# Gated projection: the last four column tiles as block products by seven multiplications, all engines in written order

## The chip, the cores and the metric

One core of a Trainium2 chip runs the whole program. The metric is the device time of one execution in microseconds (us). The engines are TensorE (PE, matrix products), VectorE (DVE, elementwise), ScalarE (ACT, activations, copies and casts), GpSimd (POOL), and the queues that issue DMAs (SP, ACT, POOL). Each engine runs its own instructions in one order and waits on semaphores for the others.

## The reference

One block of a conformer with a state-space branch: 512 tokens of 1024 features, all in float32. Cut to what matters here:

```python
h = rms_norm(x, mix_pre_g[i])
proj = h @ w_in[i]
u_glu, z, xbc, dt_raw, gates = ...           # pieces of proj
val, gt = jnp.split(u_glu + glu_b, 2, axis=-1)
v = val * jax.nn.sigmoid(gt)                 # the gated projection
v = causal_depthwise_conv(v, dw_w, dw_b)     # 31 taps
conv_out = jax.nn.silu(layer_norm(v, ln_g, ln_b)) @ pw_w + pw_b
ssm_out = ssd_branch(z, xbc, dt_raw, ...)    # 8 groups
mixed = (g_conv * conv_out + g_ssm * ssm_out) @ w_out[i]
x = x + rms_norm(mixed, mix_post_g[i])
...                                          # a gated feed-forward part
```

val and gt have 1024 columns each, 8 tiles of 128; the four last tiles of both are what the change touches.

## The kernel before

**Products.** A float32 product is made of three products of a fast type: each operand is split into a high and a low half, and `mm3` (L251 to L260) issues high x high (L253), and the two mixed ones (L255, L259). Activations are held as `hhi`/`hlo` (features x 512 tokens). Weights come in pieces of 128 x 1024 by the SP queue into `raw` (5 buffers), ScalarE casts the high half `whi` (L209), VectorE subtracts the low half `wlo` (L216); for some pieces ScalarE writes the negative high half and a POOL DMA adds the weights onto it in memory (L213, L214).

**Stages on TensorE.** val and glu of tiles 0 to 3 (on x before its normalisation, scaled afterwards by `rb`); z of group 0 with the time steps dt (`pz0`, L529); val and glu of tiles 4 to 7 (`pv4` to `pg7`): eight projections of 8 x 3 matmuls of 512 columns; then eight SSD groups. A group projects x (two tiles, `px`), B and C, transposes x (`pxT`), forms the diagonal product with the decay matrix `L`, the state product (`pSa`, `pSb`, from `xdec` and `BT`) and the part from earlier chunks. After them the gates, the pointwise product of the convolution branch, the output projection and the feed-forward part. The pointwise product and gate-up are already block products: both operands are cut in 2 x 2 blocks, sums and differences of blocks are multiplied, and seven products of 256 columns take the place of eight.

**The convolution.** Each of the 8 gated tiles `v` needs 31 taps into a tile `a`, all on VectorE (L521). They fill VectorE between other work, from a list (`taps`) that the stages draw from by fixed numbers (`TAPS`, `TAPS_GLU`).

**The time steps.** `time_steps` (L446) makes dt on VectorE. `running_sums` (L465) multiplies by a triangle (`pcs`) and by ones (`pend`) on TensorE, then transposes the running sums (`pT`) and writes them to memory (`scr`); `make_L` (L489) reads them back spread over partitions by a POOL DMA, masks them on GpSimd with affine_select (L496), and ScalarE takes 16 exponentials per group (L503).

**Order.** TensorE's and VectorE's order follows the program with edges put in by hand (`not_before`, `issue_after`, `by_table`, `keep_in_program_order`); `by_table` keeps ScalarE's calls in program order where they need tables, so that the 16 exponentials of a group stand together. The gate-up part has written orders for VectorE and ScalarE.

Of the kernel before, what the change touches and what calls it, by code (L numbers as in the profile page):

```python
# [1797 lines left out]
```

## Time and profile before

| | us |
|---|---|
| three runs | 1012.22, 1013.33, 1015.75 |
| median | 1013.33 |
| the profiled execution | 1013.44 |
| its span in the profile | 1011.7 |

The span runs from the first to the last instruction; the 1.7 us beside it lie around the program. The profile's stages by TensorE's start times:

| start us | stage |
|---|---|
| 51.08 | z of group 0 and dt |
| 63.81 | val and glu, tiles 4 to 7 |
| 108.04 | SSD group 0 |
| 129.80 | group 1 |
| 170.04 | group 2 |
| 480.00 | gates, z of the last groups and the end of SSD |
| 600.83 | pointwise product |
| 687 | gate-up |
| 898 | down projection |

A row of the timeline has start, duration, engine, line, operation, out<-in and shape, and in brackets the idle time of the engine before it with what ended it. Durations of pipelined instructions overlap: the cost of one in a full engine is the distance from its start to the next start.

### The profile page before, as it was taken

The page shows a single profiled execution, that of the slowest core. Times are in us where ns is not written, and L with a number is a line of the kernel's source. Part 1 is how long each engine was busy: PE and PEld are TensorE (multiplying, and loading weights), DVE is VectorE, ACT ScalarE, POOL GpSimd, SP SyncE. Part 2 cuts the span into 40 slices and gives each one's busy share as a digit, 9 for nine tenths or more (in the row PEclk, how much of TensorE's full clock was granted, in tenths as well). Part 3 has the DMA queues.
Part 4 walks back from the last instruction along what each step waited for, and adds up shares of the span by engine and source line. Part 5 has one row for each costly group of instructions (what it writes and reads, how often), then busy time and mean ns, then how long its engine had stood idle before and what let it go on. Part 6 is the DMA issues. An engine that isn't in the chain of part 4 may idle for free.

```text
span 1011.7 us, 15883 instructions
## 1 busy us (share of the span) xinstructions
PE 1003.7 (99%) x6152; PEld 877.9 (87%) x6152; DVE 845.7 (84%) x1230; ACT 619.8 (61%) x1045; POOL 105.9 (10%) x138
## 2 busy tenths in 40 slices
PE   9999999999999999999999999999999999999997
PEld 7898889888888888888888889889999999998886
DVE  7899977868696779668987889779999897899984
ACT  7655774767665756573542586487666566668552
POOL 0101202020121011100110110011000000001001
PEclk9999999999999999999999999999999999999999
DMA  8567545645654466356452356734655455459622
GB/s 303 150 167 218 160 100 147 178 111 145 152 165 109 118 190 167 79 144 174 104 126 84 105 122 191 227 115 127 221 147 167 146 147 146 138 172 289 214 84 83
DMA packets 43803, 155.02 MB, mean 153 GB/s; under 512 B 5072, under 2 KB 6096, under 8 KB 42704
## 3 DMA queue, kind: packets, MB, share of 16 engines
q1 hardware_dynamic: 30672, 105.44, 30.6%
q0 software_dynamic: 11136, 43.00, 21.5%
q10 hardware_dynamic: 1920, 5.57, 1.6%
q8 instruction: 48, 0.79, 0.3%
q14 instruction: 27, 0.22, 0.1%
HBM read 149.73 MB, written 4.26 MB: 152 GB/s over the span
## 4 chain that ended last, share of the span: by engine, by line
PE 92%; DVE 4%; ACT 3%; issue 1%; POOL 0%; POOLq 0%; DVEq 0%; ACTq 0%
PE xy L259 4%; PE xy L253 4%; PE xy L255 4%; PE pso L253 3%; PE pso L255 3%; PE pso L259 3%; PE yv L259 2%; PE yv L253 2%; PE yv L255 2%; PE pz L255 2%; PE pz L259 2%; PE pz L253 2%; PE px L259 2%; PE px L253 2%; PE px L255 2%; PE pgs L259 1%
## 5 line engine op out<-in xcount | busy, mean ns | idle before, releaser
L521 DVE SCALAR_TENSOR_TENSOR a<-v,prm_t,a 128x511 f32<-128x511 f32 (+15 forms) x240 | 182.8, 765 | 14.9 <-ACT a L518 12.9
L209 ACT CAST whi<-raw 128x1024 fp32r<-128x1024 f32 x99 | 102.6, 1048 | 127.9 <-PE pso L255 36.7
L216 DVE TENSOR_TENSOR wlo<-raw,whi 128x1024 fp32r<-128x1024 f32 x58 | 70.5, 1218 | 32.9 <-ACT whi L209 32.7
L214 POOL DMA_DIRECT2D wlo<-in_w x41 | 36.5, 889 | 368.8 <-ACT wlo L213 164.5
L255 PE MATMUL pz<-wlo,hhi 128*128 128x512 f32 (+2 forms) x160 | 56.2, 351 | 0.0
L259 PE MATMUL pz<-whi,hlo 128*128 128x512 f32 (+2 forms) x160 | 56.1, 352 | 0.0
L253 PE MATMUL pz<-whi,hhi 128*128 128x512 f32 (+2 forms) x160 | 55.4, 352 | 0.0
L253 PE MATMUL px<-hhi,whi 128*128 128x512 f32 x128 | 50.2, 392 | 0.0
L253 PE MATMUL pso<-yh,whi 128*128 128x512 f32 x128 | 50.2, 395 | 0.0
L1197 ACT CAST whi_g<-raw 128x1024 fp32r<-128x1024 f32 x40 | 41.4, 1051 | 13.9 <-DVE raw L1230 7.7
L259 PE MATMUL px<-hhi,wlo 128*128 128x512 f32 x128 | 49.8, 389 | 0.0
L255 PE MATMUL px<-hlo,whi 128*128 128x512 f32 x128 | 49.8, 389 | 0.0
L255 PE MATMUL pso<-yl,whi 128*128 128x512 f32 x128 | 49.8, 390 | 0.0
L259 PE MATMUL pso<-yh,wlo 128*128 128x512 f32 x128 | 49.7, 390 | 0.0
L608 DVE SCALAR_TENSOR_TENSOR x<-px,prm_t,x 128x511 f32<-128x511 f32 (+2 forms) x48 | 34.7, 742 | 13.8 <-ACT x L606 13.8
L1202 DVE TENSOR_TENSOR wlo_g<-raw,whi_g 128x1024 fp32r<-128x1024 f32 x34 | 41.2, 1219 | 3.6 <-ACT whi_g L1197 3.6
L213 ACT ACTIVATE wlo<-whi 128x1024 fp32r<-128x1024 f32 x41 | 43.3, 1056 | 0.3
L503 ACT ACTIVATE L<-L,nacs 128x128 f32<-128x128 f32 x128 | 38.8, 389 | 1.0 <-POOL L L496 0.9
L255 PEld LDWEIGHTS pz<-wlo,hhi 128*128 128x128 f32 x160 | 30.1, 188 | 4.5 <-DVE wlo L216 0.8
L253 PEld LDWEIGHTS pz<-whi,hhi 128*128 128x128 f32 x160 | 30.2, 189 | 3.8
L259 PEld LDWEIGHTS pz<-whi,hlo 128*128 128x128 f32 x160 | 30.2, 189 | 3.7
L1197 ACT CAST chi_g<-raw 128x1024 fp32r<-128x1024 f32 x24 | 24.9, 1054 | 10.2 <-DVE raw L1230 3.4
(767 smaller groups left out, 3445.2 us busy)
## 6 DMA issues: line engine op xcount, KB each, us to landing
raw<-in_w SPq DMA_DIRECT2D x182, 512.0 KB, 4.5
wlo<-in_w POOLq DMA_DIRECT2D x41, 512.0 KB, 6.9
L<-scr POOLq DMA_DIRECT2D x8, 1024.0 KB, 8.0
wlo_g<-in_w POOLq DMA_DIRECT2D x11, 512.0 KB, 7.6
clo_g<-in_w POOLq DMA_DIRECT2D x6, 512.0 KB, 5.7
pws<-in_w POOLq DMA_DIRECT2D x8, 256.0 KB, 6.0
pw_raws<-in_w SPq DMA_DIRECT2D x4, 512.0 KB, 6.4
xr<-in_x ACTq DMA_DIRECT2D x4, 512.0 KB, 4.2
```

The source lines that it names most:

```text
L209: mark[n, c.start] = act.copy(hi[:, c], src)
L213: act.activation(lo[:, c], hi[:, c].bitcast(F32), AF.Copy, scale=-1.0)
L214: mark["lo"] = pool.dma_start(lo[:, c], w[n][:, c].bitcast(F32R), accum_op=ALU.add)
L216: mark["wlo"] = dve.tensor_tensor(out=lo[:, c], in0=src, in1=hi[:, c].bitcast(F32), op=ALU.subtract)
L253: mark["pe"] = pe.matmul(ps, lh, rh, start=start, stop=False, skip_group_check=more)
L255: pe.matmul(ps, lh, rl, start=False, stop=False, skip_group_check=more)
L259: mark["pe3"] = pe.matmul(ps, ll, rh, start=False, stop=stop, skip_group_check=more)
L503: act.activation(L[:, h, c, :], L[:, h, c, :], AF.Exp, bias=nacs[:, c, HG * g + h : HG * g + h + 1])
L521: return dve.scalar_tensor_tensor(out=va[j][:, d:], in0=vs[j][:, : T - d], scalar=col("dw_w", j * KC + KC - 1 - d), in1=va[j][:, d:], op0= ...
L608: dve.scalar_tensor_tensor(out=a[:, d:], in0=ps[:, : T - d], scalar=col("ssm_w", i * KS + KS - 1 - d), in1=a[:, d:], op0=ALU.mult, op1=ALU ...
L1197: a_ = act.copy(hi, src)
L1202: d_ = dve.tensor_tensor(out=lo, in0=src, in1=hi.bitcast(F32), op=ALU.subtract)
```

## The change

val and glu of tiles 4 to 7 are computed as block products. For each tile pair u (tiles 4 to 7), the value and gate columns are the two column halves of a block product; tokens are cut in two halves of 256, features in two halves of 512. Each pair takes seven products of 4 x 3 matmuls of 256 columns, in place of two projections of 8 x 3 of 512.

- `h_forms` makes differences of the normalised input (in place in the input tiles, which `norm_h` now normalises in place) and their high and low halves `h_t13`, `h_t42`.
- `in_blocks` makes weight sums and differences: for each u the piece itself (A), two combinations S and C, and s for two u. A, S, C are 512-wide sums in the `raw` tiles on VectorE; s starts as `sums`, fetched by two plain POOL DMAs and two accumulating ones. Fourteen pieces are cast and split instead of eight; the low half of A comes by an accumulating DMA for u = 0, 1, 3. (In names, 11, 13, 15, 17 are u = 0 to 3.)
- Partial results leave PSUM by ScalarE copies and VectorE sums of 256 columns.
- Some tiles are merged or moved to make room; pcs, pend and pT use other PSUM banks.
- All five queues get a complete written order (`ORDER_ACT`, `ORDER_DVE`, `ORDER_PE`, `ORDER_POOL`, `ORDER_SP`; `in_written_order` turns each into edges). The hand-made edges go. In the new orders the taps of two tiles alternate, 27 of the taps stand later, and the exponentials of L stand between Silu calls: 60 table loads on ScalarE where there were 28.

```diff
+GLU_STEPS = "A0 r0 A1 S0 s0 C0 f0 S1 f1 A2 r1 c0 x0 v0 y0 w0 C1 z0 A3 f2 t2 x1 v1 y1 t3 S2 w1 s1 z1 c1 C2 f3 S3 o0 x2 v2 y2 w2 C3 z2 o1 x3 v3 o2 y3 w3 z3 d0"
...
+ORDER_PE = (
...
+def in_written_order(nc, tc, orders):
...
+        for first, then in zip(order, order[1:]):
+            tc.add_manual_dep(made[engine][then], made[engine][first].name, edge, reason="order")
...
+    def h_forms():
...
+        for k in range(K2):
+            (b11, b12), (b21, b22) = [(xk[q][:, :T2], xk[q][:, T2:T]) for q in (k, K2 + k)]
+            dve.tensor_tensor(out=b11, in0=b11, in1=b12, op=ALU.subtract)
+            dve.tensor_tensor(out=b12, in0=b22, in1=b12, op=ALU.subtract)
+            dve.scalar_tensor_tensor(out=b22, in0=b22, scalar=-1.0, in1=b11, op0=ALU.mult, op1=ALU.subtract)
+            dve.scalar_tensor_tensor(out=b21, in0=b22, scalar=-1.0, in1=b21, op0=ALU.mult, op1=ALU.subtract)
+            for q, (hi, lo) in zip((k, K2 + k), both):
+                t = xk[q].rearrange("p (n t) -> p n t", n=2)
+                act.copy(hi[:, :, k], t)
+                dve.tensor_tensor(out=lo[:, :, k], in0=t, in1=hi[:, :, k].bitcast(F32), op=ALU.subtract)
...
+            if kind == "r":
...
+                for i in range(2):
+                    pool.dma_start(src[:, i], w[n + 2 * i + 1][:, :T])
+                for i in range(2):
+                    pool.dma_start(src[:, i], w[n + 2 * i + 1][:, T:], accum_op=ALU.add)
+                return
...
+                dve.tensor_tensor(out=rb_[:, :T], in0=ra[:, :T], in1=rb_[:, :T], op=ALU.add)
+                dve.tensor_tensor(out=ra[:, :T], in0=s1_, in1=ra[:, :T], op=ALU.add)
+                dve.tensor_tensor(out=ra[:, T:], in0=ra[:, :T], in1=ra[:, T:], op=ALU.add)
...
+            act.copy(hi, src)
+            if kind == "A" and u in add_lo:
+                act.activation(lo, hi.bitcast(F32), AF.Copy, scale=-1.0)
+                pool.dma_start(lo, w[n].bitcast(F32R), accum_op=ALU.add)
+            else:
+                dve.tensor_tensor(out=lo, in0=src, in1=hi.bitcast(F32), op=ALU.subtract)
...
+    def glu_f(u):
...
+        glu_product(GX[u], u, "a11", HF["b11"], True)
+        glu_product(GY[u], u, "a12", HF["b21"], False)
...
+    def glu_x(u):
+        glu_product(GX[u], u, "s2", HF["t2"], False)
+        act.copy(GD[u][0][:, h2_], GX[u])
+
+    def glu_v(u):
+        glu_product(GV[u], u, "s1", HF["t1"], True)
+        act.copy(GD[u][1][:, h2_], GV[u])
+
+    def glu_y(u):
+        d = GD[u][1][:, h2_]
+        glu_product(GX[u], u, "s3", HF["t3"], False)
+        dve.tensor_tensor(out=d, in0=GX[u], in1=d, op=ALU.add)
+        act.activation(d, d, AF.Sigmoid, scale=-1.0, bias=col("glu_b", NK + EARLY + u))
...
-                by_table(
-                    act.activation(L[:, h, c, :], L[:, h, c, :], AF.Exp, bias=nacs[:, c, HG * g + h : HG * g + h + 1])
-                )
+                act.activation(L[:, h, c, :], L[:, h, c, :], AF.Exp, bias=nacs[:, c, HG * g + h : HG * g + h + 1])
...
+    orders = ORDER_ACT, ORDER_DVE, ORDER_PE, ORDER_POOL, ORDER_SP
+    in_written_order(nc, tc, {q.engine: order for q, order in zip((act, dve, pe, pool, sync), orders)})
```

VectorE around xdec of group 0, before: the transposed x (`pxT`) is scaled into xdt, the conv taps of the two x tiles of group 1 follow in alternation, and the L product stands behind xdec.

```order
L677 TENSOR_TENSOR xdt_1354<-pxT_0_1357,dtt 128x512
L608 SCALAR_TENSOR_TENSOR x_0_1310<-px_0_1279,prm_t,x_0_1310 128x511
L608 SCALAR_TENSOR_TENSOR x_1_1348<-px_1_1316,prm_t,x_1_1348 128x511
L608 SCALAR_TENSOR_TENSOR x_0_1310<-px_0_1279,prm_t,x_0_1310 128x510
L608 SCALAR_TENSOR_TENSOR x_1_1348<-px_1_1316,prm_t,x_1_1348 128x510
L608 SCALAR_TENSOR_TENSOR x_0_1310<-px_0_1279,prm_t,x_0_1310 128x509
L608 SCALAR_TENSOR_TENSOR x_1_1348<-px_1_1316,prm_t,x_1_1348 128x509
L678 TENSOR_TENSOR y_1355<-pxT_0_1357,hp_t 128x512
L677 TENSOR_TENSOR xdt_1354<-pxT_1_1364,dtt 128x512
L678 TENSOR_TENSOR y_1355<-pxT_1_1364,hp_t 128x512
L682 TENSOR_TENSOR xdec_1356<-xdt_1354,dec 128x768
L693 TENSOR_TENSOR L_914<-L_914,pcb_1378 128x2048
```

The same place after the change:

```order
L699 SCALAR_TENSOR_TENSOR a_858<-v_396,prm_t,a_858 128x486
L398 TENSOR_TENSOR wlo_1487<-raw_1384,whi_1486 128x1024
L890 SCALAR_TENSOR_TENSOR x_0_1514<-px_0_1483,prm_t,x_0_1514 128x511
L958 TENSOR_TENSOR xdt_1558<-pxT_0_1561,dtt 128x512
L974 TENSOR_TENSOR L_1322<-L_1322,pcb_1582 128x2048
L890 SCALAR_TENSOR_TENSOR x_0_1514<-px_0_1483,prm_t,x_0_1514 128x510
L890 SCALAR_TENSOR_TENSOR x_0_1514<-px_0_1483,prm_t,x_0_1514 128x509
L958 TENSOR_TENSOR xdt_1558<-pxT_1_1568,dtt 128x512
L963 TENSOR_TENSOR xdec_1560<-xdt_1558,dec 128x768
L959 TENSOR_TENSOR y_1559<-pxT_0_1561,hp_t 128x512
```

The L product has moved ahead of xdec, the y products and the taps of the second x tile behind it.

GpSimd's queue in the changed stage (`sums_846` is the pair of sums for u = 2 and 3, L785 a plain, L787 an accumulating DMA; in brackets what the instruction waits for):

```order
L810 DMA wlo_13A<-in_w 128x1024 [waits PE_49,Activation_49]
L785 DMA sums_846<-in_w 128x512 [waits DMAHW7_49,DMAHW2_49,DVE_49]
L785 DMA sums_846<-in_w 128x512
L787 DMA sums_846<-in_w 128x512 [waits DMASW7_49]
L787 DMA sums_846<-in_w 128x512 [waits DMASW2_49,DMASW0_49]
L810 DMA wlo_17A<-in_w 128x1024 [waits DMASW3_49,DVE_49,Activation_49]
```

Before, only accumulating DMAs of whole pieces stood there. The first of the sums waits for VectorE, because it takes the buffer of the raw piece 11, which the low half of 11S (`wlo_11S`) reads last.

VectorE where it needs these sums:

```order
L634 TENSOR_SCALAR scratch<-scratch 128x128 [waits DVE_49]
L812 TENSOR_TENSOR wlo_15A<-raw_733,whi_15A 128x1024 [waits DMASW6_49,Activation_49]
L635 TENSOR_TENSOR scratch<-scratch 128x128 [waits DVE_49]
L801 TENSOR_TENSOR raw_937<-raw_935,raw_937 128x512 [waits DMAHW6_49,DMAHW5_49]
L850 TENSOR_TENSOR sg_776<-pgx_773,sg_776 128x256 [waits PE_49,Activation_49]
L637 TENSOR_SCALAR scratch<-scratch 128x128 [waits Activation_49]
L699 SCALAR_TENSOR_TENSOR a_479<-v_390,prm_t,a_479 128x510
L638 RECIPROCAL scratch<-scratch 128x128 [waits DVE_49]
L699 SCALAR_TENSOR_TENSOR a_858<-v_396,prm_t,a_858 128x511
L802 TENSOR_TENSOR raw_733<-sums_846,raw_733 128x512 [waits DMASW1_49]
```

The last row is the first that reads `sums_846`; these are new rows, between the time-step rows (`scratch`) and the first taps (`a`).

More of the change, by code (lines that the diff above doesn't have):

```diff
@@ L174, in b3 @@
     return ap.unsqueeze(len(ap.shape)).to_broadcast(list(ap.shape) + [n])
+def in_written_order(nc, tc, orders):
+    edge = mybir.DependencyInfo(mybir.DependencyClass.NoSync, mybir.DependencyReason.DATA)
+    made, count = {e: {} for e in orders}, {}
+    for ins in nc.cur_bb.bb.instructions:
+        if ins.engine in made and ins.outs and hasattr(ins.outs[0], "bass_ap"):
+            name = ins.outs[0].bass_ap.tensor.name.rpartition("_")[0]
+            n = count[ins.engine, name] = count.get((ins.engine, name), -1) + 1
+            made[ins.engine][f"{name}.{n}"] = ins
+    for engine, order in orders.items():
+        names = list(made[engine])
+        if order[0][0].isdigit():
+            spans = [[int(i) for i in span.split("-")] for span in order]
+            order = [names[i] for span in spans for i in range(span[0], span[-1] + 1)]
+        assert sorted(order) == sorted(names)
+        for first, then in zip(order, order[1:]):
+            tc.add_manual_dep(made[engine][then], made[engine][first].name, edge, reason="order")
 @with_exitstack
@@ L208, in w_part @@
         else:
-            mark[n, c.start] = act.copy(hi[:, c], src)
+            act.copy(hi[:, c], src)
         after_zz = n > 5 and ORDER[n - 2] in ZZ_LAST
@@ L416, in norm_to_all @@
         ps = aux_tile("prb")
-        with tc.issue_after(mark["pe"].ins):
-            for t in range(NT):
-                pe.matmul(ps[:, t * P : (t + 1) * P], ones, dgs[t], start=True, stop=True)
+        for t in range(NT):
+            pe.matmul(ps[:, t * P : (t + 1) * P], ones, dgs[t], start=True, stop=True)
         act.copy(rb, ps)
@@ new lines, in glu_z @@
+    def glu_z(u):
+        j = EARLY + u
+        glu_product(GX[u], u, "a22", HF["t4"], False)
+        act.activation(GD[u][1][:, h1], GX[u], AF.Sigmoid, scale=-1.0, bias=col("glu_b", NK + j))
+        convolve(j, GD[u][0], *GD[u])
+    proj_z0()
+    time_steps()
+    h_forms()
+    for i, tg in enumerate(("xdt", "y")):
+        n = seq["val", EARLY + 2] + i
+        raws[n] = early_raw[n] = ssd.tile([P, 1024], F32, tag=tg, bufs=1 + i, name=f"raw{n}")
+    glu_step = {"f": glu_f, "x": glu_x, "v": glu_v, "y": glu_y, "w": glu_w, "z": glu_z}
@@ L603, in conv4 @@
+    for key in GLU_STEPS.split():
+        u = int(key[1])
+        if key[0] in glu_step:
+            glu_step[key[0]](u)
+        elif key[0] == "o":
+            w_split(seq["x", 0] + u)
+        elif key[0] == "d":
+            running_sums()
+        elif key[0] == "c":
+            conv_some(TAPS_GLU)
+        else:
+            glu_pair(key)
     def conv4(ps, i, name):
@@ L875, in ln_mean @@
         ps = aux_tile("plm")
-        with tc.issue_after(mark["pe"].ins):
-            pe.matmul(ps, ones, vsum, start=True, stop=True)
+        pe.matmul(ps, ones, vsum, start=True, stop=True)
         return ps
@@ L888, in ln_factor @@
         ps = aux_tile("plv")
-        with tc.issue_after(mark["pe"].ins):
-            for t in range(NT):
-                pe.matmul(ps[:, t : t + 1], sqsum[:, t * P : (t + 1) * P], ones[:, :1], start=True, stop=True)
+        for t in range(NT):
+            pe.matmul(ps[:, t : t + 1], sqsum[:, t * P : (t + 1) * P], ones[:, :1], start=True, stop=True)
         act.copy(lrs, ps[:, :NT])
@@ L1254, in product @@
             cut = CUT if (u, wn, k) in CUT_GU else None
-            m = mm3(ps, wh[:, c], wl[:, c], mh[:, k], ml[:, k], start and k == 0, k == KB - 1, not start, cut)
-            if k == 0 and mark.get("chain"):
-                not_before(m, last)
+            mm3(ps, wh[:, c], wl[:, c], mh[:, k], ml[:, k], start and k == 0, k == KB - 1, not start, cut)
     xrs, xgs = {}, {}
@@ L1376, in block_kernel @@
         if (t, k) == (2, 4):
-            with tc.issue_after(mark["pe"].ins):
-                sums, others = transposed(1)
+            sums, others = transposed(1)
             sums()
```

485 lines of the change are left out of this document (211 added, 274 removed), and 224 rows, old and new, of tables (ORDER_ACT, ORDER_DVE, ORDER_PE, ORDER_POOL).

## The prediction

> **What bounds the kernel now.** I read the page's head and its chain first, then the table by stretches, then single rows.
>
> ```profile
> span 1011.7 us, 15883 instructions
> PE 1003.7 (99%) x6152; PEld 877.9 (87%) x6152; DVE 845.7 (84%) x1230; ACT 619.8 (61%) x1045; POOL 105.9 (10%) x138
> PE 92%; DVE 4%; ACT 3%; issue 1%; POOL 0%; POOLq 0%; DVEq 0%; ACTq 0%
> 63.81:108.04 44.23, 44.23 (x200) 36.48 (x198) 42.98 (x69) 28.17 (x46) 9.63 (x9) 1.00 0.80 216
> 129.80:170.04 40.24, 40.24 (x289) 35.70 (x287) 34.08 (x49) 24.58 (x46) 4.29 (x4) 1.00 0.39 109
> 170.04:221.78 51.74, 51.74 (x298) 42.95 (x296) 36.59 (x50) 34.19 (x70) 8.59 (x10) 1.00 0.51 133
> ```
>
> TensorE is busy nearly everywhere and carries 92% of the last chain, so matmul time that is taken away comes off the end, if the operands keep up. The stretches (start:end, length, then busy PE, PEld, DVE, ACT, POOL, clock, DMA share, GB/s) show the reserve. The changed stage, 63.81 to 108.04, leaves VectorE 44.23 - 42.98 = 1.25 us; later ones leave 6 and 15 us. The clock is full. So VectorE is the second limit, and it is nearly reached exactly where the change is made.
>
> **What is removed.** The first and last rows of the stage on TensorE, and two places one pair (14 products of 12 matmuls) apart in the gate-up stage, which already multiplies in blocks:
>
> ```profile
> 63.81 0.40 PE L253 MATMUL pv<-hhi,whi 128*128 128x512 f32 x1
> 108.04 0.39 PE L253 MATMUL px<-hhi,whi 128*128 128x512 f32 x1
> 725.52 0.28 PE L253 MATMUL yv<-b21h,whi_g 128*128 128x256 f32 x1
> 744.56 0.28 PE L253 MATMUL yv<-b21h,whi_g 128*128 128x256 f32 x1
> ```
>
> Between the first two lie 192 matmuls of 512 columns; eight projections of 24 take about 5.44 us each when nothing but they runs, that is 226.7 ns a matmul (44.23 less 43.5 is pcs, pend, pT and their changes of type). Between the last two lie 168 of 256 columns: 19.04 / 168 = 113.3 ns. After, 4 column pairs x 7 products x 4 x 3 = 336 matmuls of 256: 38.08 us against 43.52, **-5.44 us** if TensorE never waits.
>
> The Trainium skill, "TensorE: Matmul & The Clock Gate", section "Back-to-back issue gap", speaks against this: it gives a sustained 81 ns at 128 columns and 131 ns at 512, so a half-width matmul would cost far more than half. An estimate on the straight line between them (98 ns at 256) would make 336 short ones cost 1.3 times 192 long ones. The rows here contradict it for this kind: exactly one half.
>
> **What VectorE gains in work.** I compare its two written orders from the first v/sg product up to xdec of SSD group 0, and price the difference by start-to-start distances:
>
> ```profile
> 112.79 2.31 DVE L521 SCALAR_TENSOR_TENSOR a<-v,prm_t,a 128x511 f32<-128x511 f32 x3
> 115.02 0.74 DVE L608 SCALAR_TENSOR_TENSOR x<-px,prm_t,x 128x511 f32<-128x511 f32 x1
> 115.68 0.74 DVE L521 SCALAR_TENSOR_TENSOR a<-v,prm_t,a 128x508 f32<-128x508 f32 x1
> 118.96 1.22 DVE L216 TENSOR_TENSOR wlo<-raw,whi 128x1024 fp32r<-128x1024 f32 x1
> 120.10 0.74 DVE L521 SCALAR_TENSOR_TENSOR a<-v,prm_t,a 128x505 f32<-128x505 f32 x1
> 146.46 0.68 DVE L677 TENSOR_TENSOR xdt<-pxT,dtt 128x512 f32<-128x512 f32 x1
> 147.06 0.68 DVE L678 TENSOR_TENSOR y<-pxT,hp_t 128x512 f32<-128x512 f32 x1
> 147.66 0.95 DVE L682 TENSOR_TENSOR xdec<-xdt,dec 128x768 f32<-128x768 f32 x1
> 148.52 2.28 DVE L693 TENSOR_TENSOR L<-L,pcb 128x2048 f32<-128x2048 f32 x1
> 150.72 0.73 DVE L521 SCALAR_TENSOR_TENSOR a<-v,prm_t,a 128x494 f32<-128x494 f32 x1
> 155.10 0.42 DVE L707 TENSOR_TENSOR ptmp<-prev,cd 128x256 f32<-128x256 f32 x1
> 155.44 0.74 DVE L608 SCALAR_TENSOR_TENSOR B<-pB,prm_t,B 128x509 f32<-128x509 f32 x1
> ```
>
> A tap costs 0.74 us behind a tap of the same tile, 0.66 us in alternation; a low half of 1024 columns 1.14; a sum of 512 columns 0.60, of 256 columns 0.34 (a scalar_tensor_tensor of 256 I estimate at 0.40, keeping the 0.06 by which the 512 one exceeds its sum); the L product 2.20. The terms:
> - taps 77 to 50: 77 x 0.70 - 50 x 0.65 = -21.4
> - low halves 9 to 16: +8.0
> - weight sums of 512, 12 new: +7.2
> - low halves of t1..t4, 8 new: +4.8
> - differences of the input, 8 + 8 of 256: +5.9
> - sums out of PSUM, 12 of 256: +4.1
> - the L product, now ahead of xdec: +2.2
> - two y products and three x taps now behind it: -3.2
>
> Sum **+7.6 us**, although 27 taps leave. Against it stands what VectorE now idles in that stretch:
>
> ```profile
> 100.22 0.75 DVE L553 SCALAR_TENSOR_TENSOR v<-pv,prm_t,sg 128x512 f32<-128x512 f32 x1 [0.40 <-ACT sg L552]
> 132.06 2.32 DVE L608 SCALAR_TENSOR_TENSOR C<-pC,prm_t,C 128x511 f32<-128x511 f32 x3 [0.42 <-ACT C L606]
> 141.32 0.69 DVE L677 TENSOR_TENSOR xdt<-pxT,dtt 128x512 f32<-128x512 f32 x1 [5.53 <-PE pxT L674]
> 149.39 0.38 PE L704 MATMUL pSa<-xdec,BT 128*128 128x256 f32 x1
> ```
>
> xdec ends at 148.52. Without its 6.35 us of idle and with 7.6 more it ends at 149.8. TensorE wants it for pSa at 149.39 - 5.44 = 143.95. **VectorE would be 5.8 us late**, as much as the product saves. The lag is counted against a TensorE that never waits, so shorter waits ahead of it do not add: only the largest counts.
>
> Two things move the 5.8. First, GpSimd's affine_select:
>
> ```profile
> 100.83 2.01 POOL L496 TENSOR_SCALAR_AFFINE_SELECT L<-L 128x2048 f32<-128x2048 f32 x1 [6.88 <-DMA L<-scr]
> 100.89 2.48 DVE L521 SCALAR_TENSOR_TENSOR a<-v,prm_t,a 128x490 f32<-128x490 f32 x1
> 104.93 2.35 DVE L521 SCALAR_TENSOR_TENSOR a<-v,prm_t,a 128x487 f32<-128x487 f32 x1
> 302.18 1.83 DVE L521 SCALAR_TENSOR_TENSOR a<-v,prm_t,a 128x498 f32<-128x498 f32 x1
> ```
>
> A tap beside it takes 2.4 us instead of 0.75, so two cost 3.3 us, which is inside 148.52 already; the one of a later group costs 1.1. After, the pair falls among x0 taps and a taps: 0 to 3.3, taken 2.2, that is -1.1. The Trainium skill ("SBUF — State Buffer", section "SBUF: two separate sides") calls this an exclusive lock of a port pair between GpSimd and a VectorE operation with two SBUF inputs. By that rule the loss stays 3.3 wherever a tap stands beside the select and falls to 0 for operations that read PSUM; the sum would be 5.8 or 2.5 late.
>
> Second, the sums for tiles 6 and 7 are fetched by GpSimd, plain and then added, and their buffer comes free only behind the low half of 11S:
>
> ```profile
> 577.12 1.20 POOL L958 DMA_DIRECT2D pws<-in_w  x2
> 580.52 1.85 POOL L960 DMA_DIRECT2D pws<-in_w  x2 [2.20 <-DMA pws<-in_w]
> 602.30 1.15 POOL L958 DMA_DIRECT2D pws<-in_w  x2 [2.95 <-DVE wlo_S L981]
> 609.52 0.90 POOL L960 DMA_DIRECT2D pws<-in_w  x1 [6.08 <-DMA pws<-in_w]
> DMA to landing us min/median/max: 3.0/6.0/7.6
> ```
>
> By the same construction in the pointwise stage the second transfer starts 3.4 to 7.2 us behind the first and lands 3.0 to 7.6 us later: 6.4 to 14.8. VectorE has about 11.2 us of its own work up to the raw15 sum that needs it, so it waits 0 to 3.6 us; near the medians that is about nothing, I take +0.5.
>
> Net lag 5.2 us, bounds 2.5 to 9.4.
>
> **Edits costed at nothing.** The low half of 17A comes by cast, negative copy and an accumulating DMA, after z0's buffer:
>
> ```profile
> wlo<-in_w POOLq DMA_DIRECT2D x41, 512.0 KB, 6.9
> L213 ACT ACTIVATE wlo<-whi 128x1024 fp32r<-128x1024 f32 x41 | 43.3, 1056 | 0.3
> ```
>
> Two ScalarE steps of about 1.0 and 6.9 make 8.9; until f3's third matmul TensorE has 86 matmuls x 113.3 ns = 9.7. A slower landing costs up to 1.5, covered by VectorE's lag. pT straight behind pend waits for a ScalarE copy, at most 1 us, and lies ahead of the same lag. The early stage keeps its matmuls.
>
> **The rivals.** (1) *The lag eats the saving*, as summed: -5.44 + 5.2 = -0.2 on the profiled 1013.44, so 1013.2; its own span by the bounds is 1010.5 to 1017.4, its middle 1011 to 1015.5. For it: the stretch row with 1.25 us left. Against it: 102 us of VectorE work summed to 1% is a whole us.
>
> (2) *TensorE stays dense.* The distances are too high by 2 us, the selects fall on PSUM readers and the sums land early: lag 0 to 2, time 1008 to 1010.
>
> (3) *Slower: VectorE fills the later groups.* The 27 taps move into groups 1 to 6. Priced the same way, groups 2 to 4 hold 49.9 us of VectorE work each (12 more than now) against 51.7 of TensorE, plus 1.1 for each select; 0.7 us remain. The reserve with which VectorE runs ahead of the operands there is 6 to 13 us by the same sums. If waits for ScalarE or PSUM cost it more than about 3 us in each of five groups, 15 - 10 = 5 us come on top of (1): 1018. Below about 2.5 us a group nothing comes.
>
> (4) *Slower: ScalarE's tables.* Written order mixes exp of L with Silu:
>
> ```profile
> L503 ACT ACT_TABLE_LOAD x8 | 10.3, 1283 | 0.1
> L612 ACT ACT_TABLE_LOAD x8 | 10.3, 1283 | 3.7 <-DVE x L608 3.6
> ```
>
> All loads go from 28 to 60: 32 x 1.283 = 41 us, about 5 a group, where the row of 170.04 leaves ScalarE 51.74 - 34.19 = 17.6 us. It counts only if a load stands between the last conv tap and a Silu that pxT waits for, 1.28 us a group: 8 x 1.28 = 10, of which I let half be hidden, so 1018. The Trainium skill, "ScalarE: Activation LUTs", section "Table sets: the hidden batching unit", advises batching calls by set, which this undoes; the 1283 ns a load agree, and no row here shows the mixed order.
>
> **How the numbers follow.** Differences within 0.3% (3.0 us, 1010.3 to 1016.4) can't be told from no change. (1) 0.56, (2) 0.24, (3) 0.12, (4) 0.08. Faster takes (2) and 0.02 of (1): 0.26. Slower takes (3), (4) and 0.05 of (1): 0.25. Same 0.49. The profiled run lies 0.1 above the median; predicted 1013.1. Between 1009.0 and 1017.5 lie 8 in 10.
>
> **What would show it.** Right: one or several TensorE waits put down to VectorE (low halves of the new weights, xdec of group 0) that sum to 4 to 7 us before 155, VectorE without idle from 63 to there, products of 12 in 1.36 us, and px2 no more than 1 us earlier than 170.04. (2) would show px2 at 164 to 166; (3) waits for VectorE between 220 and 480; (4) waits for x whose Silu stands behind a table load. Wrong altogether if the block products aren't 1.36 us long or the DMA sums land later than 15 us.

## The result, and the profile after

| | runs | median us | range | span of the profiled run |
|---|---|---|---|---|
| before | 4 | 1013.01 | 1012.22 to 1015.75 | 1011.7 |
| after | 4 | 1023.96 | 1022.85 to 1029.58 | 1021.1 |

The ratio is 1.0114 with a 95% interval of 1.0072 to 1.0157: slower by 11 us, and above the predicted range. The range of after is wide because its runs differ; the profiled one is the fastest of the four. The page's head and last chain of the changed kernel:

```profile
span 1021.1 us, 16341 instructions
PE 1003.1 (98%) x6296; PEld 881.8 (86%) x6296; DVE 876.2 (86%) x1285; ACT 678.6 (66%) x1106; POOL 116.1 (11%) x145
PE 53%; DVE 2%; ACT 2%; issue 1%; POOL 0%; DMA 0%; POOLq 0%; DVEq 0%; ACTq 0%; SPq 0%
```

TensorE is as busy as before (1003.1 for 1003.7 us), but now inside a longer span. Stage by stage, from the start times of TensorE's first rows (lengths in us; e12 is the last experiment, below):

| stage | before | after | e12 |
|---|---|---|---|
| up to group 0 | 108.04 | 103.70 | 103.67 |
| group 0 | 21.76 | 21.86 | 21.86 |
| group 1 | 40.24 | 43.59 | 43.02 |
| group 2 | 51.74 | 54.18 | 51.49 |
| group 3 | 51.83 | 51.81 | 51.26 |
| group 4 | 51.88 | 53.62 | 51.62 |
| group 5 | 51.69 | 53.21 | 51.66 |
| group 6 | 51.63 | 53.22 | 51.62 |
| group 7 | 51.20 | 51.80 | 51.24 |
| gates | 120.82 | 121.64 | 121.19 |
| pointwise | 30.98 | 32.13 | 31.73 |
| output projection | 55.57 | 55.35 | 55.25 |
| gate-up and the rest | 317.56 | 318.25 | 319.35 |

Up to group 0 the change did bring 4.34 us. Then 13.76 go, 10.6 of them in groups 1, 2, 4, 5 and 6. The table of TensorE's waits after (what it waited with, for what; total us, times, longest):

```profile
PE pz L426 <- ACT z L940: 3.8, 3, 1.7
PE pC L426 <- DVE x L890: 2.6, 1, 2.6
PE pwx L426 <- DVE pd L1291: 1.3, 1, 1.3
PE pyT L1050 <- DVE y L959: 1.0, 1, 1.0
PE pxT L955 <- DVE yhl L1052: 0.8, 1, 0.8
PE pSa L985 <- DVE xdec L963: 0.2, 1, 0.2
```

Three are for ScalarE's z, in groups 2, 4 and 6; the rows for VectorE sum to 5.9 us. The stretches of groups 1, 2, 4, 5, 6 and 7 (start:end, length, then busy PE, PEld, DVE, ACT, POOL, clock, DMA share, GB/s):

```profile
125.56:169.15 43.59, 40.77 (x289) 35.58 (x288) 43.52 (x59) 35.05 (x69) 8.87 (x9) 1.00 0.58 146
169.15:223.33 54.18, 52.24 (x297) 42.79 (x296) 52.02 (x76) 48.35 (x78) 8.21 (x8) 1.00 0.40 107
275.14:328.76 53.62, 51.96 (x298) 43.10 (x296) 51.99 (x75) 43.12 (x82) 9.08 (x9) 1.00 0.41 108
328.76:381.97 53.21, 52.44 (x296) 42.94 (x295) 49.35 (x71) 36.82 (x58) 8.78 (x7) 1.00 0.66 178
381.97:435.19 53.22, 51.91 (x298) 43.10 (x297) 51.91 (x74) 38.89 (x72) 9.08 (x9) 1.00 0.40 100
435.19:486.99 51.80, 51.80 (x296) 42.89 (x295) 33.40 (x46) 26.02 (x35) 4.43 (x5) 1.00 0.62 163
```

VectorE is full or nearly so in these groups up to 6 (it idles 0.1 to 3.9 us in each) and then idles 18 us in group 7. The taps alone show why; first before (L521), then after (L699), each for groups 1 to 6 and for all behind them:

```profile
129.80:428.81 299.01, 82.90 (x108) 1.00 0.51 137
428.81:560.00 131.19, 43.40 (x60) 1.00 0.46 124
```

```profile
125.56:435.19 309.63, 139.81 (x202) 1.00 0.52 135
435.19:570.00 134.81, 2.70 (x4) 1.00 0.49 129
```

94 taps more lie in groups 1 to 6; 56 of them come from behind, where before spread 60 over group 7 and the gates. ScalarE ahead of z of group 4, and TensorE behind it:

```profile
317.09 1.28 ACT L682 ACT_TABLE_LOAD   x1
318.38 2.75 ACT L682 ACTIVATE L<-L,nacs 128x128 f32<-128x128 f32 x9
321.14 1.28 ACT L939 ACT_TABLE_LOAD   x1
322.43 0.38 ACT L939 ACTIVATE zb<-pz 128x256 f32<-128x256 f32 x1
322.71 0.38 ACT L940 ACTIVATE z<-pz 128x256 f32<-128x256 f32 x1
323.14 0.50 PE L426 MATMUL pz<-whi,hhi 128*128 128x512 f32 x1 [1.66 <-ACT z L940]
```

Nine exponentials of the next group's L stand ahead of zb and z with a table load on either side; they hold ScalarE 5.3 us, and TensorE waits for the PSUM bank that z would free.

So four theories for the 13.76 us. **A**: VectorE's backlog, made by the taps moved forward. **B**: ScalarE's order, exponentials ahead of z. **C**: the place of operands in memory, since matmuls without any wait also became longer (below). **D**: the complete written order as such costs.

### The profile page after: what moved, and what is told of

The parts are those of the page before. It is cut to its first block, busy times and chain, and to the rows that moved or that the text cites. A ratio compares the mean times of both kernels' runs of the same rounds, so it can differ in the third digit from the quotient of the medians.

```text
span 1021.1 us, 16341 instructions
## 1 busy us (share of the span) xinstructions
PE 1003.1 (98%) x6296; PEld 881.8 (86%) x6296; DVE 876.2 (86%) x1285; ACT 678.6 (66%) x1106; POOL 116.1 (11%) x145
## 4 chain that ended last, share of the span: by engine, by line
PE 53%; DVE 2%; ACT 2%; issue 1%; POOL 0%; DMA 0%; POOLq 0%; DVEq 0%; ACTq 0%; SPq 0%
PE xy L426 4%; PE xy L432 4%; PE xy L428 4%; PE yv L426 2%; PE yv L432 2%; PE yv L428 2%; PE pso L432 1%; PE pso L426 1%; PE pso L428 1%; PE pgs L432 1%; PE pgs L426 1%; PE pgs L428 1%; PE pgc L428 1%; PE pgc L426 1%; PE pgc L432 1%; PE tm_wo L426 1%
## 5 line engine op out<-in xcount | busy, mean ns | idle before, releaser
L699 DVE SCALAR_TENSOR_TENSOR a<-v,prm_t,a 128x511 f32<-128x511 f32 (+19 forms) x240 | 167.3, 754 | 0.1
L391 ACT CAST whi<-raw 128x1024 fp32r<-128x1024 f32 x91 | 94.4, 1047 | 82.1 <-PE pso L428 36.9
L398 DVE TENSOR_TENSOR wlo<-raw,whi 128x1024 fp32r<-128x1024 f32 x54 | 65.7, 1219 | 25.2 <-ACT whi L391 25.0
L396 POOL DMA_DIRECT2D wlo<-in_w x37 | 32.9, 890 | 303.1 <-ACT wlo L395 108.5
L426 PE MATMUL pso<-yhl,whi 128*128 128x512 f32 x128 | 50.8, 399 | 0.0
L432 PE MATMUL pso<-yhl,wlo 128*128 128x512 f32 x128 | 50.4, 395 | 0.0
L428 PE MATMUL pso<-yhl,whi 128*128 128x512 f32 x128 | 50.3, 394 | 0.0
L395 ACT ACTIVATE wlo<-whi 128x1024 fp32r<-128x1024 f32 x37 | 39.3, 1061 | 0.5
## 6 DMA issues: line engine op xcount, KB each, us to landing
L<-scr POOLq DMA_DIRECT2D x8, 1024.0 KB, 6.1
```

Source lines behind the costliest of these rows:

```text
L391: act.copy(hi[:, c], src)
L395: act.activation(lo[:, c], hi[:, c].bitcast(F32), AF.Copy, scale=-1.0)
L396: pool.dma_start(lo[:, c], w[n][:, c].bitcast(F32R), accum_op=ALU.add)
L398: dve.tensor_tensor(out=lo[:, c], in0=src, in1=hi[:, c].bitcast(F32), op=ALU.subtract)
L426: pe.matmul(ps, lh, rh, start=start, stop=False, skip_group_check=more)
L428: pe.matmul(ps, lh, rl, start=False, stop=False, skip_group_check=more)
```

## The experiments

Each was run beside the kernel before, which its ratio refers to; the spans are of the profiled runs.

| | what | median us (runs) | ratio, 95% interval | span |
|---|---|---|---|---|
| e1_act | exponentials further ahead of z | 1024.0 (4) | 1.0093, 1.0078 to 1.0108 | 1021.8 |
| e2_skip | ten taps less | 1023.43 (4) | 1.0096, 1.0077 to 1.0115 | 1019.2 |
| e3_place | hhi, hlo and t13 moved | 1028.88 (4) | 1.0141, 1.0118 to 1.0164 | 1026.9 |
| e4_free | no written order | 1071.62 (4) | 1.0568, 1.0547 to 1.0589 | 1072.6 |
| e5_yplace | yhl and t13 moved | 1022.67 (6) | 1.0079, 1.0065 to 1.0093 | 1020.8 |
| e6_act2 | exponentials behind z | 1024.28 (6) | 1.0099, 1.0081 to 1.0118 | 1019.8 |
| e7_spread | taps spread again | 1026.54 (5) | 1.0127, 1.0108 to 1.0146 | 1023.1 |
| e8_all | e5, e6, e7 | 1024.93 (6) | 1.0100, 1.0084 to 1.0116 | 1024.9 |
| e10_act3 | exponentials far behind z | 1027.03 (6) | 1.0128, 1.0098 to 1.0159 | 1022.7 |
| e9_both | e5, e10 and taps | 1024.53 (5) | 1.0102, 1.0077 to 1.0126 | 1022.7 |
| e11_best | e9 mended | 1016.55 (12) | 1.0015, 0.9998 to 1.0032 | 1017.3 |
| e12_gates | e11 mended | 1011.85 (9) | 0.9967, 0.9955 to 0.9979 | 1011.7 |

By these ratios e1, e2, e3, e5 to e10 can't be told from after (1.0072 to 1.0157): every interval overlaps. What a single change did is therefore read from the stages of one profiled run each; only e4, e11 and e12 differ in time. Where nothing was changed, these stages repeat to about half a microsecond, except group 1 and with it group 2 (up to 1.5 us, by the halved clock of the last section), gate-up (1.4 us, under e5) and e1's stretch up to group 0 (1.9 us).

### ScalarE's order: e1, e6, e10

e1, the piece of group 4 (groups 2 and 6 alike):

```diff
 ORDER_ACT
-L5.9 zb4_0.0 z4.0 zb4_0.1 z4.1 L5.10 zb4_1.0 whi_54.0 z4.2 whi_55.0 whi_56.0 L5.11 whi_57.0
+L5.9 L5.10 L5.11 zb4_0.0 z4.0 zb4_0.1 z4.1 zb4_1.0 whi_54.0 z4.2 whi_55.0 whi_56.0 whi_57.0
```

> Changed kernel with ScalarE's order alone mended around z of groups 2, 4 and 6: the single exponentials of L3, L5 and L7 that stand between the zb and z calls are put in front of them (six tokens moved), so no table load stands between evacuations of pz. Theory B (table loads delay the release of the pz banks): the three waits of TensorE for z (0.9, 1.7 and 1.3 us) go, span 1021.1 to about 1017.5. Theory A (VectorE's backlog sets everything, z waits only ride on it): the waits reappear as waits for VectorE, span within 1 us of 1021.

The span is 1021.8, within 1 us of after, which was A's number; but the waits did not reappear as waits for VectorE. Group 2 went from 54.18 to 52.32 us, its wait for z gone and that for y 0.7 shorter; group 4's wait grew from 1.66 to 2.3, since eleven exponentials now stand ahead of zb instead of nine. The waits for z still sum to 3.0 us. Saving table loads is not the point: what stands ahead of z is.

e6, everything behind z:

```diff
 ORDER_ACT
-y3.3 L5.1 L5.2 L5.3 L5.4 L5.5 L5.6 L5.7 L5.8 L5.9 zb4_0.0 z4.0
+y3.3 zb4_0.0 z4.0
...
-x5_0.0 whi_58.0 L5.12 L5.13 L5.14 L5.15 x5_0.1 yhl2.2
+x5_0.0 whi_58.0 L5.1 L5.2 L5.3 L5.4 L5.5 L5.6 L5.7 L5.8 L5.9 L5.10 L5.11 L5.12 L5.13 L5.14 L5.15 x5_0.1 yhl2.2
```

> ScalarE alone: the exponentials of L3, L5 and L7 that stand between zb and z of groups 2, 4 and 6 are put behind z, none ahead of it. B (ScalarE's tables): TensorE's three waits for z (0.9, 1.7 and 1.3 us, 3.8 us together) fall below 0.7 us in all, and no new one comes, since L is due a group later: span 1017 to 1018.5, time near 1020. A (VectorE's backlog): VectorE sets the pace of groups 2 to 6, so at most half of that shows in the span and waits for VectorE's tiles grow instead (pxT <- yhl, pyT <- y): span 1019 to 1021.

The waits for z vanished and 4.1 us of waits for yhl took their place (pxT, groups 5 and 7): yhl's ScalarE half now stood behind fifteen exponentials. The span, 1019.8, and the kind of the new waits are what was written down for A. But VectorE's half of yhl stood waiting for ScalarE's (3.0 us in group 5), so e6 does not part the two theories; e10 does.

e10, out of the way of both (shown against e6):

```diff
 ORDER_ACT
-x5_0.0 whi_58.0 L5.1 L5.2 ... L5.15 x5_0.1 yhl2.2
+x5_0.0 whi_58.0 x5_0.1 yhl2.2
...
+prev4.0 wlo_61.0 L5.1 L5.2 ... L5.15 whi_62.0 C5.0
```

> As e6, but the exponentials of L3, L5 and L7 (15 each) go further back, behind prev of groups 3, 5 and 7 where ScalarE idles 5 to 6 us, so that they stand neither before z nor before yhl; ScalarE's order alone. e6 took the three waits for z away and got 4.1 us of waits for yhl (pxT <- yhl) in their place, because yhl's ScalarE half then stood behind the exponentials. B (ScalarE's order): both kinds of wait go, z 3.8 us and yhl 0.8 us; groups 2, 4, 5 and 6 shorten by 4 to 5 us, span 1016.5 to 1017.5. A (VectorE, busy 51 of 52 us there, sets the pace): no more than 1.5 us, other waits for VectorE in their place, span above 1019.5.

The stretches of groups 4, 5 and 6 of e10:

```profile
281.37:333.01 51.64, 51.64 (x297) 43.18 (x296) 50.07 (x71) 36.78 (x68) 9.56 (x9) 1.00 0.40 103
333.01:385.24 52.23, 52.23 (x297) 43.02 (x295) 49.41 (x71) 35.68 (x64) 7.08 (x7) 1.00 0.66 180
385.24:436.85 51.61, 51.61 (x297) 43.18 (x296) 50.78 (x74) 31.62 (x57) 9.27 (x9) 1.00 0.42 105
```

TensorE never waits in them: 155.48 us where after had 160.05. VectorE is still full, 49 to 51 of 52 us. So in these groups it was B that cost 4.6 us, and a VectorE as full as this cost nothing there. Groups 2, 4, 5 and 6 together shortened by 5.8 us, B's forecast and more; the span, 1022.7, missed it, since the gain was lost in group 3. There the moved exponentials (255.6 to 261.3) put ScalarE's first taps and C behind them, VectorE idled 3.2 us for those taps, and C's taps on VectorE, with nine others ahead of them, came too late: one wait of 5.1 us, stage 58.66. More of that stage is below, under what was not expected.

### VectorE's backlog: e2, e7

e2 leaves out the last five of 31 taps of tiles 0 and 1 (and their tokens in VectorE's order):

```diff
-taps.extend([tap(j, d) for d in range(KC)])
+taps.extend([tap(j, d) for d in range(KC - 5 if j < 2 else KC)])
```

> Changed kernel without ten of the convolution's taps (the last five of tiles 0 and 1 are left out); VectorE has 6.5 us less to do ahead of xdec of group 0. Theory A (VectorE's backlog): the waits of TensorE for x taps (2.6) and xdec (0.2) in group 1 go, and part of the later waits for y (1.0) and yhl (0.8): span 1017 to 1018.5. Theory B: only z waits matter, the span falls by less than 1 us, since the waits in group 1 are taken by something else.

The wait of pC for x fell from 2.6 to 0.5 us and group 1 from 43.59 to 42.06: VectorE's lag there is real. In the runs that left these taps alone (e1, e3, e5, e6, e10) the same wait is 1.5 to 2.5 us. Nothing followed in later groups, and the span, 1019.2, lies between the two numbers written down, A's 1017 to 1018.5 and B's above 1020.

e7, VectorE's taps by group and ScalarE's late first taps (a2.0, a4.0 to a7.0):

```diff
 taps up to group 0, in groups 0 to 6, group 7, gates
-22 28 18 39 38 35 26 34 0 0
+22 20 18 27 27 22 18 26 20 40
```

> VectorE's order alone (with the eight first taps of ScalarE moved to where their buffers come free): the 240 taps keep their own sequence, but lie 22 up to group 0, then 20, 18, 27, 27, 22, 18, 26 in groups 0 to 6, 20 in group 7 and 40 beside the gates, where after has 22, 28, 18, 39, 38, 35, 26, 34, 0 and 0. Nothing is left out. A (VectorE's backlog): VectorE idles again in groups 2 to 6 (busy 45 of 52 us), waits for x, pd, y and yhl (8.5 - 3.8 = 4.7 us together) fall below 2 us, and the small gaps behind them too: groups 1 to 6 shorten by 3 to 6 us, span 1015 to 1018. B and C: under 1.5 us. D (the written order as such): the stages are cut by an order that suits only the backlog, other waits take their place, span above 1021.

Group 1 came down to 40.49 us (40.24 before): A, worth 3.1 us there. Groups 1 to 6 together shortened by 1.4 us only, where A had 3 to 6; the span, 1023.1, is what was written down for D, other waits in the place of the old ones. Group 4, with VectorE a fifth idle, took 53.00 (53.62 after), for it still waits 1.1 us for z:

```profile
275.12:328.12 53.00, 51.91 (x298) 43.10 (x297) 43.06 (x60) 44.60 (x83) 8.94 (x9) 1.00 0.38 100
```

Beside e10 this is the pair that decides for groups 4 to 6: relieving VectorE takes 0.9 us off them, relieving ScalarE 4.6. e7's gain was eaten by a wait of pyT for y in group 2 (3.0 us; the y products stood behind L and the last taps of tiles 0 and 1) and in the gates (124.5 for 121.6 us), where pso waited 1.6 us for VectorE's so, among the 40 taps spread beside it.

### The place of the operands: e3, e5

```diff
-hp_pool.tile([P, 80], F32, name="hT_place")
+hp_pool.tile([P, 32], F32, name="hT_place")
...
-r[:, MOV_AT // 4 + i * 4 * T : ...] for r in rooms
+r[:, at + i * 4 * T : ...] for r, at in zip(rooms, (MOV_AT // 4 + 32, MOV_AT // 4))
```

> Changed kernel with the addresses of the moving operands shifted alone: hhi and hlo by 192 bytes, h_t13 by 128, so that each lies 192 bytes off the weights modulo 512, as the gate-up operands do. Theory C (the spacing of 256-column matmuls depends on where the two operands lie): the 28 products shrink from 1.41 on average to 1.36 to 1.38 us, so 0.9 to 1.4 us in that stage, and z of group 1 (120 ns a matmul) may move too: span 1018 to 1020. Rival (traffic of VectorE and DMAs slows them): products stay at 1.41, span 1021.

Neither number came (1018 to 1020, or 1021): the span is 1026.9. The last nineteen block products got shorter (1.36 us but for one short wait, where after has 1.36 to 1.44), the first nine stayed at 1.41 to 1.42, and every 512-column matmul on hhi became longer. 48 px from one row to the next, after and e3:

```profile
125.56 0.39 PE L426 MATMUL px<-hhi,whi 128*128 128x512 f32 x1
136.45 1.03 PE L955 MATMUL pxT<-ident,x 128*128 128x128 f32 x8
```

```profile
126.27 0.39 PE L426 MATMUL px<-hhi,whi 128*128 128x512 f32 x1
137.48 1.04 PE L955 MATMUL pxT<-ident,x 128*128 128x128 f32 x8
```

10.89 us against 11.21: 226.9 and 233.5 ns each. The same numbers turn up for yhl, which the change had put elsewhere by merging tiles. e5 moves yhl, and t13, by 128 bytes, and nothing else:

```diff
-yhl[:, i * 4 * T : (i + 1) * 4 * T]
+yhl[:, 32 + i * 4 * T : 32 + (i + 1) * 4 * T]
```

> The halves of the gated projection's output (yhl) stand 128 bytes further on in their own buffer, so that they lie at the same place modulo 512 as the hi and lo weights, as they did in the kernel before; the halves t1 and t3 of the GLU's moving operands also go 128 bytes on, to distance 192. No instruction, order or wait changes. C (place of the operands): the output projection's matmuls go from 234.5 to 228.5 ns, 384 of them, 2.3 us; products of t1 and t3 from 1.41 to 1.36-1.38 us, 0.3 to 0.4 us; 2.6 us in all, span 1018.5, time near 1021. A, B and D: no change, span 1021. If the place were without effect on 512-wide matmuls and it is the merged tile or its partition stride that costs, 234.5 stays.

48 pso from one row to the next before, after and in e5:

```profile
468.46 0.39 PE L253 MATMUL pso<-yh,whi 128*128 128x512 f32 x1
479.34 0.59 PE L728 MATMUL pYa<-prev,C 128*128 128x256 f32 x2
```

```profile
475.13 0.40 PE L426 MATMUL pso<-yhl,whi 128*128 128x512 f32 x1
486.32 0.59 PE L1009 MATMUL pYa<-prev,C 128*128 128x256 f32 x2
```

```profile
473.79 0.39 PE L426 MATMUL pso<-yhl,whi 128*128 128x512 f32 x1
484.67 0.59 PE L1009 MATMUL pYa<-prev,C 128*128 128x256 f32 x2
```

10.88, 11.19, 10.88 us. Eight such runs (384 matmuls) make 2.5 us, and group 5, group 7 and the gates, which hold three quarters of them, each became 0.5 to 0.6 us shorter; the products went from 39.53 to 39.16. C is shown, 2.5 + 0.4 us. In e5's span it shows with 0.3 only, because group 1 and gate-up took 1.5 and 1.4 us more in its profiled run. In group 1 the clock was halved for 3.4 us (last section). In gate-up ptr waited 1.5 us, since one tiny operation of GpSimd ahead of it (rs_b, 128 x 1) took 2.67 us and not 0.86. It did so in e3, e5, e8, e11 and e12, which all have moved operands, but not in e9, which has them too; the cause is open.

### The order as such: e4

```diff
-in_written_order(nc, tc, {q.engine: order for q, order in zip((act, dve, pe, pool, sync), orders)})
+pass
```

> Changed kernel without any written order: the block products stay, each engine follows the scheduler's own order (program order with no edges by hand; 67 table loads). Rival D (the written order as such costs the time, not the products): span 1008 to 1016. Theories A and B: the same work and no fewer table loads, so the span is 1021 or more, with waits for ScalarE and VectorE in every group.

About 48 us slower than after: pcs waits 10.7 us for the time steps, pxT 8.2 for yhl, and the clock is 0.979. Without any order the block products are far worse. That leaves out the hand-made edges too, so it does not by itself say what a complete order costs; e12, whose order is just as complete as after's, shows that it need cost nothing. What remains of D is what e7 showed, that a place changed in such an order can make a new wait elsewhere.

### All together: e8, e9, e11, e12

> e5, e6 and e7 together. If the three causes add (2.6 + 3.3 + 3 to 6 us off 1022.9): 1011 to 1014, level with the kernel before at 1013 to 1014. If one hides another (VectorE and ScalarE wait at the same stages): 1015 to 1018. The product saving that is left on TensorE is 3.9 us, and 1.4 us of it still go to products at 1.41 us.

Neither number came; the span is 1024.9. The kinds of wait that e6 and e7 had left are here too (yhl 4.1, y 2.1, so 2.0), while groups 3, 4 and 6 are at 51.25 to 51.63: the gains are in it and the faults with them, with more waiting in the pointwise stage (35.6 for 32.1 us).

e9 takes e10's exponentials and these taps, with y ahead of L in group 1:

```diff
 taps up to group 0, in groups 0 to 6, beside group 7, its scan, pso, behind
-22 28 18 39 38 35 26 34 0 0 0 0
+22 20 14 29 29 24 18 24 17 23 6 14
```

> e5's places, e10's exponentials, and the taps spread again: 22 up to group 0, then 20, 14, 29, 29, 24, 18, 24 in groups 0 to 6, 17 beside group 7's projections, 23 beside its scan, 6 beside the output projection's first sums and 14 behind them (e7 and e8 had 40 evenly beside the gates and cost 2.5 us there, pso <- so 2.0), and in group 1 the two y's stand before L (e7, e8: pyT <- y 3.0 and 2.1 us). If the causes are VectorE's and ScalarE's orders plus the places: waits of TensorE up to 560 us under 2 us in all, group stages at 51.2 to 52 us, span 1008 to 1012, below the kernel before by 0 to 5 us. If TensorE's waits only move again, as in e6 and e8: span 1015 to 1022.

Groups 3 to 7 stand at 51.2 to 51.7 us without a wait, as forecast; the span, 1022.7, missed the forecast. Group 2 took 59.95: ScalarE reached the first taps of tiles 2 and 3 before VectorE had freed their buffers, 4.8 us, and C behind them held pz for 5.9.

```diff
 ORDER_ACT (e11)
-x2_1.1 a2.0 a3.0 L2.7
+yhl0.1 a2.0 a3.0 L3.0
 taps beside group 7 and the gates
-17 23 6 14
+20 17 8 7 8
```

> e9 with its two own faults taken out: ScalarE's first taps of tiles 2 and 3 stand behind C of group 2 (in e9 they waited for VectorE's last taps of tiles 0 and 1 and held B, C and so pz: 5.9 us, stage 59.95 for 51.7), and the taps beside group 7 and the gates lie 20, 17, 8, 7 and 8 (e9: yhl of group 7 late, and vsum 1.2 us). Same computation, nothing left out. If VectorE's and ScalarE's written orders and the places are the whole of the loss: group 2 at 51.7 to 52.5, gates 63.2 to 64, sum 9 to 11 us off e9's 1022.7: span 1011 to 1014, that is level with the kernel before (1011.1 to 1013.9) and 7 to 10 us below after. If waits only move from stage to stage (the place where they end is a matter of the order as a whole): above 1016.

Level with the kernel before: 1.0015, and group 2 at 51.50. Left were the gates (123.72, after 121.64; the expectations' 63 to 66 us are of a shorter stretch) and the pointwise stage (34.85, a copy of pd standing behind whi_101S, which waits for a transfer, and a halved clock behind that wait).

```diff
 ORDER_ACT (e12)
-whi_101S.0 pd2_0.0 pd1_0.1
+pd2_0.0 pd1_0.1 whi_101S.0
 taps beside group 7, its scan, behind wlo_84, pso, behind
-20 17 8 7 8
+22 9 10 8 11
```

VectorE's sums of pd move likewise.

> e11 with its last waits taken up: beside group 7's scan 9 taps instead of 17, 10 of them where VectorE idled 5.7 us behind wlo_84 (in e11 y, yl and so of group 7 came late: pyT 1.15 us longer, pso <- yhl 1.1), and in the pointwise stage the copy pd of tile 1 stands ahead of whi_101S, which waits for a transfer (pwx <- pd 2.1 us in e11, 1.3 in after), on VectorE likewise. If these waits are what holds e11 level with the kernel before: gates 66.1 to 63.2-64.5, pointwise 34.9 to 31.5-33, span 3 to 5 us below e11's (1011.1 to 1017.3 in its runs): 1007 to 1013, and the median 1 to 4 us below the kernel before. If they only move: as e11, 1011 to 1017.

The page's chain of e12, its waits on TensorE over 0.3 us, and its stretches of groups 1 and 4:

```profile
PE 91%; DVE 2%; ACT 2%; issue 2%; DMA 1%; POOL 1%; SPq 0%; POOLq 0%; ACTq 0%; DVEq 0%
```

```profile
PE ptr L1504 <- ACT mg L1491: 1.7, 2, 1.5
PE pcb L972 <- ACT C L894: 1.3, 1, 1.3
PE warm_ps L510 <- DVE woken L505: 1.0, 1, 1.0
PE pC L426 <- DVE x L890: 0.6, 1, 0.6
PE pwx L426 <- DVE pd L1291: 0.5, 1, 0.5
```

```profile
125.53:168.55 43.02, 40.98 (x289) 35.57 (x287) 38.31 (x51) 34.74 (x69) 9.65 (x7) 1.00 0.54 151
271.30:322.92 51.62, 51.62 (x297) 43.17 (x296) 45.92 (x64) 38.36 (x71) 8.99 (x9) 1.00 0.41 103
```

e12 computes all that after does, and is faster than the kernel before by 0.33% (0.21 to 0.45%), about 3.3 us. The chain is TensorE's again. Its profiled run was its longest (1013.46 us); in it group 1 still takes 2.8 us more than before (1.3 of them a wait of pcb for ScalarE's C) and gate-up 1.8 (1.5 of them the wait of ptr named under e5). So its column of stages sums to the same span as before; the 3.3 us are those of the medians.

## Why the prediction was wrong

**Up to group 2 it held, but for the sizes of a product and of the waits.** Forecast were 38.08 us for the 336 matmuls. The first of them after the change, and the first row behind them:

```profile
63.35 0.28 PE L426 MATMUL pgx<-hhi,whi_11A 128*128 128x256 f32 x1
102.88 0.38 PE L653 MATMUL pcs<-scratch,tri 128*128 128x128 f32 x2
```

39.53 us, 117.6 ns each and not 113.3, so the saving was 4.0 and not 5.44. By the prediction's own sign ("if the block products aren't 1.36 us long") this alone was a miss: they took 1.36 to 1.44. By e3 the place of the operands (C) accounts for some 0.9 of the 1.45 us, those of the last nineteen products; what the first nine lost is open. The end of xdec of group 0 was forecast at 149.8 - 1.1 + 0.5 = 149.2; it ended at 148.28:

```profile
147.32 0.96 DVE L963 TENSOR_TENSOR xdec<-xdt,dec 128x768 f32<-128x768 f32 x1
148.42 1.10 PE L985 MATMUL pSa<-xdec,BT 128*128 128x256 f32 x4 [0.21 <-DVE xdec L963]
```

From the stage's start to there VectorE idled 0.8 us for a weight piece and 0.3 for the sums (0.5 forecast), no more. TensorE's waits from the stage's start to 155 sum to 2.8 us (4 to 7 forecast), nearly all one step earlier, at pC. px2 started at 169.15, 0.9 us earlier than before: "no more than 1 us" was right. It was right in part by luck: the saving was 1.4 us smaller than summed and the waits 2.4 us.

**The select.** Of the 3.3 us that a pair of affine_selects can cost, the prediction let 2.2 stand. After:

```profile
124.15 2.01 POOL L676 TENSOR_SCALAR_AFFINE_SELECT L<-L 128x2048 f32<-128x2048 f32 x1 [4.64 <-DMA L<-scr]
124.67 2.01 DVE L699 SCALAR_TENSOR_TENSOR a<-v,prm_t,a 128x495 f32<-128x495 f32 x1
128.10 2.39 POOL L676 TENSOR_SCALAR_AFFINE_SELECT L<-L 128x2048 f32<-128x2048 f32 x1 [1.94 <-DMA L<-scr]
128.55 2.46 DVE L699 SCALAR_TENSOR_TENSOR a<-v,prm_t,a 128x492 f32<-128x492 f32 x1
```

Taps of 2.01 and 2.46 us for 0.72, each ending 0.52 us behind its select: 3.0 us, nearly the whole 3.3. With 0.8 us more here and 0.6 more of idle, and xdec 0.9 us early all the same, VectorE's own work was some 2.3 us less than the sum had it. The Trainium skill, "SBUF — State Buffer", section "SBUF: two separate sides", calls this an exclusive lock for operations with two SBUF inputs; the trace agrees, the tap that starts during a select is the one that stretched.

**The step that failed is the last one, where rivals (1), (3) and (4) were given one chance each.** They do not exclude one another. (1) used up most of the saving by group 2, as forecast (0.9 us were left), and (4) came on top, with part of (3), and with a cost that had no term.

- Rival (4) had the right mechanism at another place: the exponentials stand ahead of z, not ahead of the Silu that pxT waits for, and it cost 4.6 us in groups 4 to 6 (e10): 3.0 of waits for z, 0.8 of one for yhl, the rest around them. Its condition, a load between the last conv tap and a Silu that pxT waits for, shows in no wait; nor was the cost 1.28 us in every group, but 0.9 to 1.7 us in three of them. It had 0.08.
- Rival (3) had VectorE's fill right (49.9 of 51.7 us forecast in groups 2 to 4; 52.0 of 54.2, 51.0 of 51.8 and 52.0 of 53.6 measured), and its words wrong: not 27 taps move into groups 1 to 6 but 94, most of them forward from group 7 and the gates. Its condition, VectorE itself waiting more than 3 us in each of five groups, did not come: it idled 2.2, 0.8, 1.6, 3.9 and 1.3 us in groups 2 to 6, and e10 ran three full groups without a wait of TensorE. The backlog cost in group 1 (3.1 us by e7), and a wait of 1.0 in group 2.
- **"Some tiles are merged or moved"** had no term at all. It cost 2.5 us in the output projection's matmuls (e5) and some 0.9 in the products (e3).

Summed on the two profiles: -4.3 up to group 0, +5.9 of waits for VectorE, +3.8 for z, +2.5 for yhl's place, and 1.5 that I did not trace, against 9.4 measured between the spans. Of the 5.9, 1.3 are the wait of pwx for pd in the pointwise stage, behind all taps. The mechanisms for slower were named, but each was held to be worth 5 us and alone: 1018 for either. Added up they would have given 1013 + 5 + 5 = 1023, near the measured 1024, though the parts measured were others.

## What to carry to other kernels

When an engine is kept busy by work without a date (here the taps), where a new order puts it counts more than its amount: take the count by stage from both orders before pricing anything. Ask of each rival whether it excludes the others; costs at different stages of the same critical engine add. And an order that is written out anew is mended wait by wait: e6, e10, e9 and e11 each removed what they aimed at and showed the next, and only e12, with most of it mended, paid.
